# All transposed column pairs of a kernel's second half as seven products of sums, in two passes over token groups

## The chip, the cores and the metric

The kernel runs on one core of one Trainium2 chip. A time is device microseconds from start to end of one execution. The engines are TensorE (PE in the profile; PEld its weight loads), VectorE (DVE), ScalarE (ACT), GpSimd (POOL) and SyncE (SP), whose queue issues nearly all DMA transfers.

## What is computed

One layer of a streaming encoder for 2048 prompt tokens (positions 0 to 2047) and 64 sample tokens of a stream with 4096 past positions, all in float32 with model width 1024:

```
h = rmsnorm(x, norm_g) @ w_in                  # 1024 x 6144 columns: qa ka va za qb kb vb zb (512 each), ga gb (1024 each)
oa = differential attention(rmsnorm(qa), rmsnorm(ka), va)   # 4 heads, two 64-wide halves, chunk mask, linear bias
ob = retention(qb, kb / sqrt(128), vb)         # 4 heads of 128, chunks of 64, a running state
oa = rmsnorm(oa) * (1 - lam_init) * silu(za);  ob = rmsnorm(ob) * silu(zb)
y = x + (sigmoid(ga) * (oa @ w_oa) + sigmoid(gb) * (ob @ w_ob)) @ w_out
```

Keys, values and the retention state are outputs too.

## The kernel before

**Matmuls in parts.** Each float32 operand is kept as a high part in the PE's round float type and a low part, the difference (tiles `xh`, `xl`, `wh`, `wl`); a product is three matmuls, high by high, high by low and low by high. A matmul has 128 x 128 weights and 256, 288 or 512 moving columns. For a weight block, a DMA lands 256 KB in a staging tile `ws` (three of them), ACT casts it to `wh` (L727), and POOL or DVE subtracts to get `wl` (L748). Twelve `w` buffers make six high/low pairs.

**Two halves.** The first half projects 1024 prompt tokens and, for the columns of attention, the sample tokens. The second, which the change touches, has the other 1024 prompt tokens and, for the columns of the pairs, the 64 sample tokens: 1088 columns, taken as two token halves of 544, each in two groups of 256 and 288. The quarters A11, A12, A21, A22 of x are named by token half and by 512-row half of the contraction; S1 to S4 are their sums. x is scaled, transposed and split by the end of the first half and stays in SBUF.

**Columns of the second half.** va, ka, qa and vb are made with tokens on the partitions (`natural`, `mm_group`, L1137). The other 4096 columns make 16 pairs of 128-column blocks, with columns on the partitions, and are stored to DRAM (qbT, kbT, zaT, zbT, gaT, gbT). Eleven of the pairs go through `transposed`, eight block products per pair and group; the last five through `quad` (L1566), phase by phase: for each of seven products, all five pairs, and both token groups with the same weights. A phase's x sum is formed by POOL (`x_again`), stored to DRAM (`xd`), loaded to `xraw` and split by ACT and DVE (`x_pass`, L1527, L1530). Sums of weight blocks were formed in the first half and stored (`wsum`) for these five pairs. The products come out of PSUM as sums: ACT copies (L1593) or DVE adds to an SBUF tile `u` (L1586).

**Beside it.** Attention of both halves (`qk_block` L1880 and L1881; softmax L1889, L1920, L1942; `at_pv` L1970 to L2008) and retention run between the projection's blocks. After the last pair the output follows: gated heads by the two output weights (L2673 to L2679), then the final product (L2801 to L2803). Their weights and inputs are loaded and split during the last pairs.

**What sets the order.** The program is written by a planner of generator tasks with priorities: each keeps clocks of the engines (`self.pe`, `act`, `dve`, `pool`, `dma`) and yields a time or a condition; the planner emits the instruction of the first task that may go. Each engine, and the SP queue, executes in the order of emission. `lighter` gives an operation to DVE or POOL by whose planned clock is behind.

**Small roots.** `rsqrt_small` takes the inverse root of up to 8 values per partition: two ACT operations (L381, L382) and three on DVE (L385 to L387). `rms_t` normalises attention's output; one 1 x 256 cast (L1713) is DVE's.

## Time and profile before

| | |
|---|---|
| times of three runs | 1881.78 to 1882.8 us, median 1882.35 |
| profiled execution, span | 1880.5 us |
| PE busy | 1866.5 us, 99% |
| DVE, ACT, POOL busy | 71%, 52%, 36% |
| DMA | 340.07 MB, mean 181 GB/s |
| granted TensorE clock | 1.000 |

The span runs from the first to the last instruction of the profiled execution. The profile groups instructions by line, engine, operation and tile; a time behind a group is its busy time and the mean of one, or, where three numbers stand with slashes, the least, the median and the largest in ns. A busy PE is not PE at its peak: matmuls overlap, so the spacing of their starts counts, not the duration of one.

### The profile page before, as it was taken

What the parts mean: (1) busy time and instruction counts of PE and PEld (TensorE: products, weight loads), DVE (VectorE), ACT (ScalarE), POOL (GpSimd) and SP (SyncE); (2) the same over time, 40 slices, a digit from 0 to 9 for tenths busy, and PEclk for the clock granted to TensorE, in tenths of its full rate; (3) what the DMA queues carried; (4) which work ended last, traced back from release to release, by engine and by line L of the source; (5) the groups of instructions that cost most, each with busy time, mean ns of one, the idle gap of its engine ahead of it and who ended that gap; (6) DMA issues with size and microseconds to landing.
All of it is one profiled execution on the core that took longest, in us unless ns stands there. A gap on an engine that the chain in (4) does not pass through costs nothing.

```text
span 1880.5 us, 33007 instructions
## 1 busy us (share of the span) xinstructions
PE 1866.5 (99%) x11090; PEld 1645.2 (87%) x11090; DVE 1331.2 (71%) x3112; ACT 975.8 (52%) x2266; POOL 679.2 (36%) x728
## 2 busy tenths in 40 slices
PE   9999999999999999999999999999999999999999
PEld 7788888888888889888988889999999999998887
DVE  6765857558585677787587777677875769887664
ACT  6434545554434566556465655556666446564221
POOL 2420356555552122023210344243224555432442
PEclk9999999999999999999999999999999999999999
DMA  7664555666867967556523659446437988886542
GB/s 257 215 176 125 160 164 171 180 198 196 246 183 192 262 190 191 155 171 173 140 73 96 176 135 244 120 129 155 120 112 234 262 253 249 260 260 216 161 158 77
DMA packets 402555, 340.07 MB, mean 181 GB/s; under 512 B 85329, under 2 KB 348625, under 8 KB 401362
## 3 DMA queue, kind: packets, MB, share of 16 engines
q1 hardware_dynamic: 402386, 337.97, 61.6%
q8 instruction: 87, 1.43, 0.3%
q14 instruction: 82, 0.67, 0.1%
HBM read 218.27 MB, written 118.75 MB: 179 GB/s over the span
## 4 chain that ended last, share of the span: by engine, by line
PE 84%; DMA 6%; DVE 4%; SPq 2%; ACT 1%; issue 1%; POOL 1%; DVEq 0%; ACTq 0%; POOLq 0%
PE mm L1137 30%; PE mm L989 8%; PE tp L989 4%; PE at L1992 3%; PE s L1880 2%; PE s L1881 2%; PE s L989 2%; PE pv L1972 2%; PE pv L1971 2%; PE pv L1970 2%; PE s L2803 1%; PE s L2802 1%; PE s L2801 1%; SPq L280 1%; PE pv L2258 1%
## 5 line engine op out<-in xcount | busy, mean ns | idle before, releaser
L748 POOL TENSOR_TENSOR wl<-ws,wh 128x512 fp32r<-128x512 f32 x107 | 148.1, 1395 | 256.5 <-ACT wh L727 185.2
L1137 PE MATMUL mm<-wh,xh 128*128 128x512 f32 x504 | 203.0, 403 | 0.0
L1137 PE MATMUL mm<-wl,xh 128*128 128x512 f32 x504 | 197.9, 393 | 0.4 <-POOL wl L748 0.4
L1137 PE MATMUL mm<-wh,xl 128*128 128x512 f32 x504 | 198.2, 393 | 0.0
L1137 PE MATMUL mm<-xh,wh 128*128 128x288 f32 (+2 forms) x544 | 179.8, 331 | 0.0
L1137 PE MATMUL mm<-xh,wl 128*128 128x288 f32 (+2 forms) x544 | 175.5, 323 | 0.0
L1137 PE MATMUL mm<-xl,wh 128*128 128x288 f32 (+2 forms) x544 | 175.5, 323 | 0.0
L1920 ACT ACTIVATE row<-row,a_mx 128x1024 f32<-128x1024 f32 (+7 forms) x144 | 149.7, 1042 | 12.0 <-DVE a_mx L1899 12.0
L2008 DVE TENSOR_TENSOR atl<-at,ath 128x512 fp32r<-128x512 f32 (+1 forms) x144 | 92.5, 658 | 77.0 <-ACT ath L2006 76.9
L2006 ACT CAST ath<-at 128x512 fp32r<-128x512 f32 (+1 forms) x144 | 79.2, 565 | 106.5 <-PE at L1992 106.0
L856 POOL TENSOR_TENSOR wl<-ws,wh 128x256 fp32r<-128x256 f32 x64 | 54.9, 858 | 198.0 <-ACT wh L847 197.7
L1747 POOL TENSOR_TENSOR r_y<-r_y,r_sq 128x256 f32<-128x256 f32 x32 | 30.4, 949 | 237.2 <-DVE r_sq L1744 154.1
L1137 PEld LDWEIGHTS mm<-wh,xl 128*128 128x128 f32 x504 | 94.6, 188 | 21.5
L1137 PEld LDWEIGHTS mm<-wl,xh 128*128 128x128 f32 x504 | 95.0, 188 | 18.5 <-POOL wl L748 0.9
L1137 PEld LDWEIGHTS mm<-wh,xh 128*128 128x128 f32 x504 | 94.8, 188 | 17.8 <-DVE raw L1308 0.2
L1137 PEld LDWEIGHTS mm<-xh,wh 128*128 128x128 f32 x544 | 102.4, 188 | 7.2
L1137 PEld LDWEIGHTS mm<-xl,wh 128*128 128x128 f32 x544 | 102.5, 188 | 6.9
L1137 PEld LDWEIGHTS mm<-xh,wl 128*128 128x128 f32 x544 | 102.3, 188 | 6.7
L1889 DVE CUSTOM_DVE_ANT_0 row<-s,dfar 128x512 f32<-128x512 f32 (+2 forms) x141 | 87.0, 628 | 24.0 <-PE s L1881 18.1
L1942 DVE SCALAR_TENSOR_TENSOR row<-row,a_w 128x1024 f32<-128x1024 f32 (+5 forms) x88 | 96.5, 1102 | 0.0
L1880 PE MATMUL s<-K,q 128*128 128x512 f32 (+3 forms) x240 | 90.5, 379 | 1.1 <-DVE a_acc L1889 1.1
L727 ACT CAST wh<-ws 128x512 fp32r<-128x512 f32 x111 | 67.7, 619 | 41.3 <-PE mm L1137 9.8
(543 smaller groups left out, 5959.4 us busy)
## 6 DMA issues: line engine op xcount, KB each, us to landing
ws<-in_w_in_dram SPq DMA_DIRECT2D x155, 256.0 KB, 3.4
q<-qT SPq DMA_DIRECT2D x128, 128.0 KB, 4.0
K<-kT SPq DMA_DIRECT2D x48, 256.0 KB, 4.5
V<-vN SPq DMA_DIRECT2D x24, 512.0 KB, 5.7
...
wz<-in_w_in_dram SPq DMA_DIRECT2D x32, 256.0 KB, 4.1
row<-in_cache_k_T_dram SPq DMA_DIRECT2D x32, 256.0 KB, 3.1
row<-in_cache_v_diff_dram SPq DMA_DIRECT2D x32, 256.0 KB, 3.6
```

Of the source, the lines that this page charges most:

```text
L727: self.nc.scalar.copy(h, st)
L748: eng.tensor_sub(l, st, h.bitcast(F32))
L856: nc.gpsimd.tensor_sub(l[:, cs], src, h[:, cs].bitcast(F32))
L989: nc.tensor.matmul(ps, w[:, c], xs[x][c], start=bool(tag) and c == 0 and i == 0, stop=c == 3 and i == 2, skip_group_check=True)
L1137: nc.tensor.matmul(ps, p, q, start=c == 0 and i == 0, stop=c == KC - 1 and i == 2)
L1880: nc.tensor.matmul(ps, q1s, kk, start=True, stop=False)
L1889: nc.vector.tensor_tensor_reduce(out=row[:, k0:k0 + n], in0=ps, in1=tab, scale=-SLOPES[h], scalar=3.0e38, op0=ALU.add, op1=ALU.min, accum_ ...
L1920: nc.scalar.activation(u, u, AF.Exp, bias=mx, scale=-1.0, accum_out=lp[:, k:k + 1])
L1942: nc.vector.scalar_tensor_tensor(out=u0, in0=u1, scalar=w[:, 0:1], in1=u0, op0=ALU.mult, op1=ALU.add)
L1992: nc.tensor.transpose(at[:, w:w + 128], src, self.ident)
L2006: nc.scalar.copy(ah[:, :w], at[:, :w])
L2008: nc.vector.tensor_sub(al[:, :w], at[:, :w], ah[:, :w].bitcast(F32))
```

## The change

All 16 pairs go through the new `third` (matmuls at L1524 of the changed kernel), in two passes: all pairs for the token group of 256, then all pairs for the group of 288. A pair and group takes seven products of twelve matmuls in the order of the table `THIRD`: the weight block or sum, the x quarter or sum, the accumulator (a to d), and what has to be read out of the accumulator first. Three products are added onto an accumulator that already holds another. Each pass loads, casts and splits all its weight blocks, 224 in all; the sums come from DRAM (`wsum`, now for 16 pairs in eight stores each) straight into the `wl` tile, without a staging tile. Low parts of these blocks are DVE's or POOL's, whichever clock is behind, until the output weights are being prepared (`self.wo` is set), and DVE's from then on.

The four x sums of each group are formed at staging (`x_form`, on DVE or POOL) and stored to `xsum`; x of the second group is stored split to `xg` and its place reused; `x_flow` loads and splits the operands of each pass. va of the second half comes first, as two groups of 256 columns. Retention's second half is started after four pairs of each pass, a part of it each time. `rsqrt_small` becomes one POOL power, and in `rms_t` the L1713 cast goes, with ACT casting the squares in place of squaring twice.

```diff
+THIRD = [("b11", "A11", "a", None, "t_p1"), ("t2", "S2", "b", None, "t_p6"), ("b21", "A12", "a", "p1", "t_p2"),
+         ("t3", "S3", "c", None, "t_p7"), ("t1", "S1", "d", None, "t_p5"), ("t4", "A22", "c", "u3", "t_p4"),
+         ("b22", "S4", "d", "c22", "t_p3")]
+SUMS = ("S1", "S3", "S2", "S4")
 WIDTH = (256, 288)
+HANDOVER = [("S2", 1, 0), ("A12", 0, 0), ("S3", 0, 1), ("S1", 1, 1), ("A22", 0, 2), ("S4", 1, 2)]
...
+        self.wsum = tc.dram_tile([16, 4, 128, 4, 128], F32, name="wsum")
+        self.xsum = tc.dram_tile([2, 4, 128, 4, 288], F32, name="xsum")
+        self.xg = tc.dram_tile([2, 128, 2, KC, 288], F32, name="xg")
...
     def rsqrt_small(self, ms, n, ready):
-        nc = self.nc
-        sp = self.sp
         r = ms.shape[0]
...
-        nc.scalar.activation(y, ms, AF.Ln)
-        nc.scalar.activation(y, y, AF.Exp, scale=-0.5)
-        self.A(n, ready, 40)
-        yield self.A(n, 0.0, 40)
-        nc.vector.scalar_tensor_tensor(out=t, in0=y, scalar=-0.5, in1=y, op0=ALU.mult, op1=ALU.mult)
-        nc.vector.tensor_mul(t, t, ms)
-        nc.vector.scalar_tensor_tensor(out=y, in0=t, scalar=1.5, in1=y, op0=ALU.add, op1=ALU.mult)
-        for _ in range(3):
-            self.tr = self.V(70, self.act)
+        y = self.sp.tile([128, 8], F32, tag="sm_y", name="sm_y")[:r, :n]
+        self.nc.gpsimd.tensor_tensor(y, ms, self.power[:r, :n], op=ALU.pow)
+        self.pool = max(self.pool, ready) + 350 + 165 * n
+        self.tr = self.pool + LAT
+        yield self.tr
...
+    def x_form(self, g, tiles, t):
+        nc = self.nc
+        a11, a12, a21, a22 = tiles
+        yield t
+        for k, (out, one, two, op) in enumerate(((a22, a22, a21, "tensor_add"), (a21, a11, a21, "tensor_sub"),
+                                                 (a11, a22, a11, "tensor_sub"), (a12, a12, a11, "tensor_sub"))):
+            eng, cost = self.lighter()
+            getattr(eng, op)(out, one, two)
+            t = cost(1024, t)
+            self.spawn(self.x_put(g, k, out, t), 1, "w")
+            yield t - LAT - PACE
+
+    def x_put(self, g, k, out, t):
+        yield t + g * k * PARK
+        t = self.st(self.xsum[g, k, :, :, 0:256], out.rearrange("p (c t) -> p c t", c=4), 1 << 19)
...
     def next_load(self, c0, kind):
         for shape, src in self.w_source(c0, kind):
-            yield from self.take("ws")
-            st = self.sb(self.wp, shape, "ws")
-            self.wst.append((st, self.ld(st, src, 1 << 18), shape))
+            st = None
+            if kind != "pair" or src.tensor is self.i["w_in"].tensor:
+                yield from self.take("ws")
+                st = self.sb(self.wp, shape, "ws")
+            wx = kind is True and self.spare
+            tag = yield from self.either(2, "w", *(("wx",) if wx else ()))
+            h, l = (self.sb(self.spare if tag == "wx" else self.wp, shape, tag, n, F32R) for n in ("wh", "wl"))
+            raw = l.bitcast(F32) if st is None else st
+            self.wst.append((raw, st is not None, h, l, self.ld(raw, src, 1 << 18), (tag, tag)))
             yield self.pe
     def next_piece(self, kind):
         self.npiece += 1
         yield lambda: len(self.wst) > 0
...
+        raw, staged, h, l, t, tags = self.wst.pop(0)
         if t > self.pe:
             yield t
-        self.nc.scalar.copy(h, st)
+        self.nc.scalar.copy(h, raw)
         t = self.A(512, max(self.pe, t))
-        if kind is True:
+        if kind is False:
+            new = [[h[:, 0], l[:, 0], None, (), t], [h[:, 1], l[:, 1], None, tags, t]]
+        elif kind is True:
             new = [[h[:, 0], l[:, 0], None, tags, t]]
...
         else:
             new = [[h, l, None, tags, t]]
         self.wq += new
...
+        self.spawn(self.next_low(kind, raw, staged, h, l, t, new), 0, "w")
+        yield self.act - PACE
+    def next_low(self, kind, raw, staged, h, l, t, new):
+        eng, cost = self.nc.gpsimd, self.G
+        if kind == "pair":
+            yield t - LAT
+            eng, cost = self.lighter() if self.wo is None else (self.nc.vector, self.V)
+        eng.tensor_sub(l, raw, h.bitcast(F32))
         t = cost(512, t)
-        self.give("ws", t)
+        if staged:
+            self.give("ws", t)
         for u in new:
             u[2] = t
+        yield self.pe
...
+    def x_flow(self):
+        self.xop, self.xlast = [{}, {}], {}
+        self.passed = False
+        xh, xl = self.xnext[0]
+        yield lambda: len(self.xt_ready) == 8
+        for k, (b, j) in (("A11", (0, 0)), ("A12", (0, 1)), ("A22", (1, 1))):
+            self.xop[0][k] = (*(x[:, b, 4 * j:4 * j + 4] for x in (xh, xl)), 0.0)
+        yield lambda: "kqv11" in self.done
+        for k, x in enumerate(self.xnext[1]):
+            t = self.st(self.xg[k], x.bitcast(F32), 1 << 21)
+        yield lambda: self.seg1_done is not None
+        yield max(self.seg1_done, t + LATE)
+        for k, name in enumerate(("S2", "S1", "S4")):
+            self.spawn(self.x_half(0, name, *(x[:, 1152 * k:1152 * k + 1024] for x in self.xroom[1])), 0, "w")
+        self.x_whole("A11", *(x[:, 3456:4608] for x in self.xroom[1]))
+        yield lambda: "nat1" in self.done
+        yield self.marks["nat1"] + LAT
+        yield from self.x_half(0, "S3", *(x[:, 2048:3072] for x in self.xroom[0]))
+        for name, seg, k in HANDOVER:
+            yield lambda: name in self.xlast
+            yield self.xlast[name]
+            parts = [x[:, 1152 * k:1152 * k + 1152] for x in self.xroom[seg]]
+            if name[0] == "A":
+                self.x_whole(name, *parts)
+            else:
+                self.spawn(self.x_half(1, name, *parts), 0, "w")
+        yield lambda: len(self.xop[1]) == 7
+        self.passed = True
+
+    def x_whole(self, name, h, l):
+        b, j = (int(k) - 1 for k in name[1:])
+        for k, x in enumerate((h, l)):
+            t = self.ld(x.bitcast(F32), self.xg[k, :, b, 4 * j:4 * j + 4].rearrange("p c t -> p (c t)"), 589824)
+        self.xop[1][name] = (*(x.rearrange("p (c t) -> p c t", c=4) for x in (h, l)), t)
+
+    def x_half(self, g, name, h, l):
+        nc = self.nc
+        n = WIDTH[g]
+        raw = l.bitcast(F32)
+        t = self.ld(raw.rearrange("p (c t) -> p c t", c=4), self.xsum[g, SUMS.index(name), :, :, 0:n], 2048 * n)
+        yield t
+        for c in range(2):
+            sl = slice(2 * n * c, 2 * n * c + 2 * n)
+            nc.scalar.copy(h[:, sl], raw[:, sl])
+            t = self.A(2 * n, self.pe)
+            yield t
+            eng, cost = self.lighter()
+            eng.tensor_sub(l[:, sl], raw[:, sl], h[:, sl].bitcast(F32))
+            t = cost(2 * n + 100, t)
+        self.xop[g][name] = (*(x.rearrange("p (c t) -> p c t", c=4) for x in (h, l)), t)
+
+    def third(self, g, dst, d0, scale, grouped, last):
+
+        nc = self.nc
+        n = WIDTH[g]
+        q = {"g": g, "n": n}
+        bank = {}
+        for name, op, b, after, fin in THIRD:
+            yield lambda: len(self.wq) > 0 and self.wq[0][2]
+            wh, wl, t, tags, _ = self.wq.pop(0)
+            yield lambda: op in self.xop[g]
+            xh, xl, tx = self.xop[g][op]
+            if after is None:
+                tag = yield from self.either(1, "mm", *(("tp",) if self.wo is None else ("s", "at")))
+                bank[b] = (self.psum(tag)[:, :n], tag)
+            else:
+                yield lambda: after in q
+                t = max(t, q[after])
+            ps, tag = bank[b]
+            if max(t, tx) > self.pe:
+                yield max(t, tx)
+            for c in range(4):
+                for k, (w, x) in enumerate(((wh, xh), (wh, xl), (wl, xh))):
+                    nc.tensor.matmul(ps, w[:, c], x[:, c], start=after is None and c == 0 and k == 0,
+                                     stop=c == 3 and k == 2, skip_group_check=True)
+                    t = self.P(n)
+                if c == 1:
+                    yield self.pe
+            for tag2 in tags:
+                self.give(tag2, t)
...
+            self.spawn(getattr(self, fin)(q, ps, tag, t, dst, d0, scale, grouped), 0, "w")
             yield self.pe
...
+    def t_p1(self, q, ps, bank, t, dst, d0, scale, grouped):
+        q["a"], tag = q["at"] = yield from self.q_ev(q["n"])
+        yield t
+        q["p1"] = self.q_copy(q["a"], ps, scale, q["n"], t)
+
+    def t_p6(self, q, ps, bank, t, dst, d0, scale, grouped):
+        yield lambda: "p1" in q
+        q["b"], q["bt"] = yield from self.q_ev(q["n"])
+        yield max(t, q["p1"])
+        q["u2"] = t = self.q_scaled(q["b"], ps, q["a"], scale, q["n"], t)
+        self.give(q["at"][1], t)
+        self.give(bank, t)
+
...
+    def t_p7(self, q, ps, bank, t, dst, d0, scale, grouped):
+        yield lambda: "u2" in q
+        q["c"], q["ct"] = yield from self.q_ev(q["n"])
+        yield max(t, q["u2"])
+        q["u3"] = self.q_scaled(q["c"], ps, q["b"], scale, q["n"], t)
+
...
+    def t_p5(self, q, ps, bank, t, dst, d0, scale, grouped):
+        yield lambda: "u3" in q
+        ev, tag, t = yield from self.t_out(q, "c", ps, max(t, q["u3"]), scale)
+        q["c22"] = t
...
-        later = [(vb, lambda half: self.natural(half, self.fin_vb(), False, True), True)]
-        plain = [(c0, lambda half, a=a: self.transposed(*a), False) for c0, a in again[:PLAIN]]
-        c0s, args = zip(*again[PLAIN:])
-        seqs = [first + early + seq, [plain[0], wide[0], plain[1], wide[1], wide[2], m0, m1, plain[2], plain[3],
-                                      *later, (None, "nat"), (None, "ret"), *plain[4:],
-                                      (c0s, lambda half: self.quad(args), "quad")]]
+        later = (vb, lambda half: self.natural(half, self.fin_vb(), False, True, True), True)
+        second = [(va + 256 * g, lambda half, g=g: self.natural(half, self.fin_va(g), True), False) for g in range(2)]
+        second += [*wide[1:], m0, m1, later, (None, "nat")]
+        for g in range(2):
+            for k, (c0, a) in enumerate(again):
+                second.append((c0, lambda half, g=g, a=a, k=k: self.third(g, *a, g == 0 and k == 15), "pair"))
+                if k == 3:
+                    second.append((None, ("ret", "rest")[g]))
+        seqs = [first + early + seq, second]
```

**SP where the second half starts.** Ahead of the first attention loads (K, q and V are attention's operands, ws weights, vN and kT outputs kept in DRAM). Before:

```order
L280 DMA q<-qT_58 64x2x256 x2
L280 DMA ws<-in_w_in_dram 128x2x256
L285 DMA vN_61<-thi 128x512
L285 DMA out_v_prompt_dram<-raw 128x512
L285 DMA vN_62<-tlo 128x512
L285 DMA oaT<-r_o 128x256
```

With the change:

```order
L287 DMA xsum<-row 512x1x256 x2
L287 DMA xsum<-xT 512x1x256 x2
L287 DMA vN_61<-thi 128x2x256
L287 DMA out_v_prompt_dram<-raw 128x2x256
L287 DMA gbT<-ev 128x2x256
L287 DMA vN_62<-tlo 128x2x256
L287 DMA xsum<-row 512x1x256
L282 DMA dnear<-in_c_dnear_dram 128x512
L287 DMA vN_61<-thi 128x2x256
L287 DMA out_v_prompt_dram<-raw 128x2x256
L282 DMA K<-kT_59 64x1024
L282 DMA K<-kT_60 64x1024
```

Stores of the x sums stand between and ahead of these loads.

**SP in the last pairs.** wst are output weights, z and on the output's inputs, gaT and gbT results. Before:

```order
L280 DMA xraw<-xd 128x2176
L280 DMA z<-zaT 128x2x264
L280 DMA on<-oaT 128x2x264
L280 DMA ws<-wsum 128x4x128
L280 DMA z<-zbT 128x2x264
L280 DMA on<-obT 128x2x264
```

With the change:

```order
L282 DMA ws<-in_w_in_dram 128x4x128
L287 DMA gaT<-ev 128x4x8
L287 DMA gaT<-ev 128x256
L282 DMA wst<-in_w_o_ret_dram 128x2x256
L282 DMA ws<-in_w_in_dram 128x4x128
L282 DMA wst<-in_w_o_ret_dram 128x2x256
L282 DMA wl<-wsum 128x512
L287 DMA gbT<-ev 128x4x8
L287 DMA gbT<-ev 128x256
L282 DMA ws<-in_w_in_dram 128x4x128
```

A weight load, of one block, now stands between the stores of every result.

**DVE in the last pairs.** ev and u are evacuations, on the gated heads. Before:

```order
L1586 TENSOR_TENSOR ev<-s,u_16727 128x288
L2479 TENSOR_TENSOR w_o_retl_16953<-wst,w_o_reth_16952 128x2x256
L1586 TENSOR_TENSOR ev<-at,u_16726 128x256
L1586 TENSOR_TENSOR ev<-at,u_16727 128x288
L2479 TENSOR_TENSOR w_o_diffl_16951<-wst,w_o_diffh_16950 128x2x256
L1586 TENSOR_TENSOR ev<-mm,u_16726 128x256
L1586 TENSOR_TENSOR ev<-mm,u_16727 128x288
```

With the change:

```order
L1593 TENSOR_TENSOR ev<-mm,ev 128x288
L770 TENSOR_TENSOR wl<-ws,wh 128x512
L770 TENSOR_TENSOR wl<-wl,wh 128x512
L1593 TENSOR_TENSOR ev<-s,ev 128x288
L770 TENSOR_TENSOR wl<-wl,wh 128x512
L2586 TENSOR_TENSOR on<-on,z 128x528
L1593 TENSOR_TENSOR ev<-at,ev 128x288
L770 TENSOR_TENSOR wl<-wl,wh 128x512
L1593 TENSOR_TENSOR ev<-at,ev 128x288
L2586 TENSOR_TENSOR on<-on,z 128x528
```

Low parts of the weights, before mostly on POOL, now stand between DVE's evacuations.

366 lines of the change are left out of this document (104 added, 262 removed).

## The prediction

> **What bounds the kernel now.** I read the page's busy times and its chain first, then TensorE's waits, then the stretches.
>
> ```profile
> PE 1866.5 (99%) x11090; PEld 1645.2 (87%) x11090; DVE 1331.2 (71%) x3112; ACT 975.8 (52%) x2266; POOL 679.2 (36%) x728
> ...
> PE 84%; DMA 6%; DVE 4%; SPq 2%; ACT 1%; issue 1%; POOL 1%; DVEq 0%; ACTq 0%; POOLq 0%
> ```
> ```profile
> PE at L2679 <- DVE ogl L2630: 1.7, 2, 1.3
> PE tp L1880 <- DMA q<-qT: 1.1, 1, 1.1
> ```
>
> TensorE is busy for 99% of the span, and its longest waits, the two rows above, are 1.7 and 1.1 us. So the time is the number of matmuls times their spacing, and a change gains what it takes from that sum and loses what it adds in waits. Where waits could come is read from the stretches (us; then busy time and instructions of PE, PEld, DVE, ACT, POOL; granted clock, DMA share, GB/s):
>
> ```profile
> 600.00:640.00 40.00, 36.89 (x229) 32.65 (x228) 22.23 (x77) 21.01 (x54) 6.28 (x5) 1.00 1.02 273
> ...
> 1720.00:1760.00 40.00, 40.00 (x175) 32.48 (x174) 33.19 (x41) 13.94 (x24) 19.15 (x12) 1.00 0.69 233
> 900.00:1417.00 517.00, 515.91 (x3397) 471.80 (x3397) 380.64 (x1071) 301.79 (x652) 152.72 (x216) 1.00 0.51 136
> 1417.00:1524.00 107.00, 107.00 (x856) 106.97 (x855) 76.00 (x124) 54.86 (x106) 55.30 (x39) 1.00 0.86 251
> ...
> 1560.00:1600.00 40.00, 40.00 (x330) 40.00 (x330) 36.72 (x64) 24.01 (x62) 22.70 (x20) 1.00 0.75 228
> ...
> 1640.00:1680.00 40.00, 40.00 (x330) 40.00 (x329) 35.99 (x65) 25.93 (x67) 19.16 (x15) 1.00 0.93 285
> ```
>
> Only 600 to 640, where the second half starts, loses PE time (3.1 us), and there the DMA engines are full. DVE at 92% (1560 to 1600) and 285 GB/s (1640 to 1680) cost nothing. The clock is 1.00 throughout.
>
> **TensorE's sum.** The spacing of matmuls comes from the starts in the timeline, for the plain projection and for the seven-product form that five pairs already have:
>
> ```profile
> 684.55 0.39 PE L1137 MATMUL mm<-wh,xl 128*128 128x512 f32 x1
> ...
> 688.03 0.40 PE L1137 MATMUL mm<-wh,xl 128*128 128x512 f32 x1
> ```
> ```profile
> 1433.05 0.28 PE L1566 MATMUL s<-xh,wh 128*128 128x256 f32 x1
> ...
> 1434.46 0.30 PE L1566 MATMUL s<-xh,wh 128*128 128x288 f32 x1
> ...
> 1436.06 0.28 PE L1566 MATMUL at<-xh,wh 128*128 128x256 f32 x1
> ```
>
> Fifteen steps of 512 columns take 3.48 us, 232.0 ns each; in 1720 to 1760, 175 of them give 228.6. I take 230. Twelve steps of 256 columns take 1.41 us, 117.5 ns each; twelve of 288 take 1.60 us, 133.3 each. So a narrow matmul costs a little more per column than a wide one, and the saving is smaller than a count of columns says.
>
> Removed with the eleven plain pairs (24 matmuls to each output block and group): 480 of 512 columns, 1056 of 288, 96 of 256. The first value projection turns 192 of 512 into 384 of 256. The five old product pairs had 420 of 256 and 420 of 288; sixteen now have 1344 of each. Net: 512, minus 672; 256, plus 1212; 288, minus 132. That is -672 x 230 + 1212 x 117.5 - 132 x 133.3 = -154.6 + 142.4 - 17.6 = **-30 us** (-29 at 228.6, -31 at 232.0). The rest of PE's work stays.
>
> **The last stretch.** On PE, attention now ends after 126 of the 224 product blocks, so 98 blocks stand with little beside them, and the last 40 or so with only the output's preparation. The old phases used each weight block for both groups, 24 matmuls or 3.01 us; a block now lasts 12 matmuls, 1.60 us in the second pass, and every weight is loaded, cast and split a second time.
>
> ```profile
> ws<-wsum SPq DMA_DIRECT2D x20, 256.0 KB, 4.9
> ```
> ```profile
> 1462.96 5.85 DMA ws<-wsum
> ```
> ```profile
> L727 ACT CAST wh<-ws x29: 604/620/636, 1420.8 to 1508.7; 128x512 fp32r<-128x512 f32 x29
> ```
> ```profile
> L748 DVE TENSOR_TENSOR wl<-ws,wh x4: 675/687/1453, 1430.8 to 1476.9; 128x512 fp32r<-128x512 f32 x4
> ```
>
> There are six high/low buffer pairs, 6 x 1.60 = 9.6 us round. A trip is landing 4.9, cast 0.62, low part 0.69, use 1.60: 7.8 us, so a landing may be 6.7 us before PE waits. At 261 GB/s one took 5.85, in the chain's row. Between the first output-weight load and the last pair weight, SP's order now has 130 transfers, 23.6 MB, beside 40 x 1.60 = 64 us of PE; before, 89 and 21.8 MB in some 70 us of 1417 to 1524. At the best rate shown, 285 GB/s, 23.6 MB take 83 us. SP says the same:
>
> ```profile
> 1456.16 2.63 SPq L285 DMA_DIRECT2D gbT<-ev  x4
> ...
> 1458.90 0.52 SPq L280 DMA_DIRECT2D ws<-wsum  x1
> ```
>
> At 0.52 to 0.66 us an issue, 130 take 68 to 86 us, and a store that waits for its evacuation holds the weight loads queued behind it. The loads start up to 9.6 us before their block. So the stall is between 0 (loads and stores spread over the earlier blocks) and 83 - 64 = 19 us; I take the middle, **+9**: nothing says that either the spreading or the lateness is complete.
>
> DVE has every low part here: 7 x 0.69 and five evacuations of 0.43 make 7.0 us per pair against 11.2 of PE, for six pairs 42 of 64 us, with ten output-weight low parts (6.9) and some gating 55. It fits, unless POOL runs beside it:
>
> ```profile
> 1455.16 0.71 DVE L1530 TENSOR_TENSOR xl<-xraw,xh 128x544 fp32r<-128x544 f32 x1
> ...
> 1456.16 1.50 DVE L1530 TENSOR_TENSOR xl<-xraw,xh 128x544 fp32r<-128x544 f32 x1
> ...
> 1457.02 1.79 POOL L748 TENSOR_TENSOR wl<-ws,wh 128x512 fp32r<-128x512 f32 x1
> ...
> 1457.58 0.41 DVE L1586 TENSOR_TENSOR ev<-at,u 128x256 f32<-128x256 f32 x1
> ```
>
> A subtraction of two SBUF tiles doubles beside a POOL one, and the evacuation from PSUM doesn't. Sixteen POOL operations of 1.8 us cover 29 of the 64 us, so some 19 of 42 low parts cost 0.8 more: 55 + 15 = 70, 6 us over. That lies within the 0 to 19 and isn't added.
>
> [...]
>
> **Attention with the first pass beside it.** The plain work beside attention was 480 x 230 + 1056 x 133.3 + 96 x 117.5 = 262 us; now it is 112 x 1.41 + 14 x 1.60 = 180, so attention's 517 us become 435. DVE's 380.6 of them gain 18 pair-passes of five evacuations,
>
> ```profile
> L1586 DVE TENSOR_TENSOR ev<-mm,u x14: 406/432/457, 1450.9 to 1525.5; 128x256 f32<-128x256 f32 x7, 128x288 f32<-128x288 f32 x7
> ```
>
> 90 x 0.43 = 38 us, and 25 low parts of 0.7 to 1.5, some 25; they lose about 28 (below, and the old sums' low parts). That is 416 of 435 us, 95%, above the 92% that the trace shows as free. Price: 0 if DVE's lead holds, 22 if the last 5% is never filled; I take **+5**, near the free end, since a stretch at 92% lost nothing.
>
> **The start of the second half.** 4.2 MB of x sums and 4.7 MB of split x are stored between loads that arrive just in time:
>
> ```profile
> 595.53 6.04 DMA q<-qT
> 601.60 4.09 DMA q<-qT
> 605.69 7.50 DMA qbT<-ev
> ```
>
> 8.9 MB at 273 GB/s are 33 us of DMA; about half meets the full 40 us, and the later stretch has room. Price 0 to 16; I take **+4**, because the second group's sums are spread out and stores wait for nobody. The sums' forming replaces 160 small POOL operations of the old re-forming, and POOL is 36% busy: nothing.
>
> **Small roots.** Fifty-one times two ACT and three DVE operations become one POOL power, for which before has no row; the cast goes too.
>
> ```profile
> L382 ACT ACTIVATE sm_y<-sm_y x51: 205/209/212, 78.8 to 1262.6; 128x8 f32<-128x8 f32 x32, 128x4 f32<-128x4 f32 x16, 64x8 f32<-64x8 f32 x2, 64x4 f32<-64x4 f32 x1
> ```
> ```profile
> L386 DVE TENSOR_TENSOR sm_t<-sm_t,ms x51: 154/167/1225, 82.3 to 1263.1; 128x8 f32<-128x8 f32 x32, 128x4 f32<-128x4 f32 x16, 64x8 f32<-64x8 f32 x2, 64x4 f32<-64x4 f32 x1
> ```
> ```profile
> L1713 DVE CAST r_hi<-r_sq x32: 280/282/1107, 621.7 to 1420.7; 1x256 fp32r<-1x256 f32 x32
> ```
> ```profile
> L1747 POOL TENSOR_TENSOR r_y<-r_y,r_sq x32: 725/740/1775, 627.0 to 1429.9; 128x256 f32<-128x256 f32 x32
> ```
>
> 51 x 3 x 0.167 = 26 us leave DVE and 32 x 0.28 = 9 more, about 28 of the 35 beside attention. A power takes between 0.167 (DVE on the same eight values) and, at ten times POOL's 256-value product, 7 us; the shape is small, so I take 1 us. The chain it replaces is 2 x 0.21 + 3 x 0.17 = 0.9 us, and nobody on PE waited for it: **0**. At 7 us, 51 cost POOL 357 us and its low parts would be late (a rival below).
>
> **Sum.** 1880.5 - 30 + 9 + 5 + 4 = 1868.5 us of span. The median, 1882.35, lies 1.85 over the profiled span: **1870 us**.
>
> **Rivals.** (a) All the new waits stay hidden: 1882.35 - 30 = 1852. For it: PE lost nothing at 92% DVE or 285 GB/s. Against it: both limits are now exceeded on the estimates above, for 64 us and longer.
>
> (b) The last stretch is starved: 19 + 5, and the start 8: 1882.35 - 30 + 32 = 1884, no change.
>
> (c) Slower: the accumulators. Three of a pair's seven products go into a bank that ACT or DVE must have read, and between lies one block, 1.41 us. Before, the evacuation came late without harm:
>
> ```profile
> 1455.44 0.27 PE L1566 MATMUL at<-xh,wl 128*128 128x256 f32 x1
> ...
> 1457.58 0.41 DVE L1586 TENSOR_TENSOR ev<-at,u 128x256 f32<-128x256 f32 x1
> ```
>
> From the product's last start to the evacuation's end are 2.55 us, 1.14 more than the cover. There are 32 pair-passes, so 96 such places; some 54 have attention's matmuls between, but the 42 of the last 14 pairs stand alone: at 1.14 each 48 us, 1882.35 - 30 + 48 + 4 = 1904. It decides from 26 / 42 = 0.62 us each. Against it: that row's evacuation stood behind a low part of 1.50 us, which is the exception.
>
> (d) The change doesn't do what it says: the power is near 7 us, or narrow matmuls fed from two passes don't keep 117.5 ns; half the saving gone, 1870 + 15 = 1885.
>
> **How the numbers follow.** Forecast 0.39, (a) 0.21, (b) 0.15, (c) 0.19, (d) 0.06. A difference of 0.2%, 3.8 us, is what a measurement can tell from none: 1878.6 and 1886.1. Faster: the forecast, (a), and a few hundredths of (b), 0.62; same: the rest of (b) and half of (d), 0.16; slower: (c) and the other half, 0.22. The range runs from (a), 1852, to 1894, short of (c). The forecast alone spans 1860 to 1878.
>
> **What would show it.** PE's matmul count up by 408 at unchanged spacing; blocks of 1.41 and 1.60 us. In the last stretch, PE waits named for DVE's low parts, ACT's casts or weight loads, some 9 us in all, with DMA near 285 GB/s; if the waits name evacuations instead, (c) is right. Beside attention, DVE at 90% or more with short waits. The forecast is wrong if PE loses over 28 us, or under 8, in all.

## The result, and the profile after

The changed kernel took 1928.68 us (median of four executions, 1925.45 to 1935.29), the kernel before 1882.41 beside it: 1.0248 times as long, interval 1.0234 to 1.0263. The forecast was 1870, its range 1852 to 1894. It is slower, and the sign was wrong.

The first two rows are the page's busy times and its chain; then come TensorE's longest waits (us in total, times, longest), and four stretches in the columns that the prediction used.

```profile
PE 1869.5 (97%) x11498; PEld 1661.5 (86%) x11498; DVE 1378.1 (71%) x3043; ACT 1016.8 (53%) x2257; POOL 825.8 (43%) x724
...
PE 77%; DVE 10%; DMA 6%; issue 2%; ACT 2%; POOL 2%; SPq 1%; DVEq 0%; ACTq 0%; POOLq 0%
```
```profile
PE s L1844 <- DVE a_acc L1853: 10.7, 10, 5.8
PE mm L1160 <- DVE tlo L1413: 5.2, 1, 5.2
...
PE s L1844 <- DMA q<-qT: 2.6, 1, 2.6
```
```profile
600.00:640.00 40.00, 27.14 (x176) 25.32 (x174) 19.81 (x44) 9.48 (x25) 9.29 (x6) 0.83 0.99 292
640.00:680.00 40.00, 36.19 (x259) 34.09 (x260) 28.02 (x90) 24.98 (x57) 7.04 (x6) 0.96 0.92 242
...
1480.00:1520.00 40.00, 36.11 (x242) 34.97 (x241) 25.68 (x44) 22.91 (x42) 9.61 (x7) 0.91 0.98 286
1520.00:1560.00 40.00, 35.50 (x249) 34.45 (x248) 30.22 (x47) 23.19 (x43) 13.00 (x9) 0.96 1.01 282
```

The number of matmuls rose by 408, as forecast. PE's share fell from 99 to 97%, DVE's share of the chain rose from 4 to 10%, and the granted clock, 1.00 throughout before, is 0.83 in one stretch and 0.91 in another. The spacing that the sum was made with held. In attention, beside the first pass, and in the last pairs:

```profile
1137.94 0.28 PE L1524 MATMUL mm<-xh,wh 128*128 128x256 f32 x1
...
1139.36 0.28 PE L1524 MATMUL tp<-xh,wh 128*128 128x256 f32 x1
...
1435.78 0.29 PE L1524 MATMUL mm<-xh,wl 128*128 128x288 f32 x1
...
1437.38 0.29 PE L1524 MATMUL mm<-xh,wl 128*128 128x288 f32 x1
```

Twelve steps take 1.42 and 1.60 us, against 1.41 and 1.60 before. So TensorE's own work did get shorter by about 30 us, and what is slower is what it loses between.

**Where it loses.** I put all matmuls of the program in their order, each at the undisturbed spacing of its form, and compared that with the starts in the trace. What the difference grows by in a stage is what TensorE lost there, by waiting or by a low clock. *Start* is the stage in which the second half begins (trace time about 590 to 760 of the changed kernel), *attention* the stage in which attention runs beside the pairs (about 900 to 1440), *last pairs* the pairs behind it (to about 1570). In us:

| | start | attention | last pairs | elsewhere | all |
|---|---|---|---|---|---|
| before | 4.4 | 2.7 | -0.3 | 16 | 23 |
| after | 28.6 | 31.9 | 15.4 | 22 | 98 |

75 us more are lost: 24 at the start, 29 beside attention, 16 in the last pairs, 6 elsewhere, of which some 5 fall in the first 100 us. 75 - 30 = 45, and 46.3 were measured.

### The profile page after: what moved, and what is told of

Read it like the earlier page. It is cut to its first block, busy times and chain, and to the rows that moved or that the text cites. A ratio compares the mean times of both kernels' runs of the same rounds, so it can differ in the third digit from the quotient of the medians.

```text
span 1927.7 us, 34579 instructions
## 1 busy us (share of the span) xinstructions
PE 1869.5 (97%) x11498; PEld 1661.5 (86%) x11498; DVE 1378.1 (71%) x3043; ACT 1016.8 (53%) x2257; POOL 825.8 (43%) x724
## 4 chain that ended last, share of the span: by engine, by line
PE 77%; DVE 10%; DMA 6%; issue 2%; ACT 2%; POOL 2%; SPq 1%; DVEq 0%; ACTq 0%; POOLq 0%
PE mm L1160 13%; PE mm L1012 9%; PE mm L1524 8%; PE tp L1012 4%; PE at L1956 2%; PE s L1012 2%; DVE row L1853 2%; PE tp L1524 2%; PE s L1844 2%; DMA ws<-in_w_in_dram 2%; PE s L1845 2%; DVE row L1906 2%; PE pv L1936 1%; DMA wl<-wsum 1%; PE pv L1935 1%
## 5 line engine op out<-in xcount | busy, mean ns | idle before, releaser
L1160 PE MATMUL mm<-wh,xh 128*128 128x512 f32 (+1 forms) x568 | 217.8, 384 | 7.4 <-DVE tlo L1413 5.2
L1160 PE MATMUL mm<-wl,xh 128*128 128x512 f32 (+1 forms) x568 | 211.6, 373 | 2.3 <-POOL wl L770 2.3
L1160 PE MATMUL mm<-wh,xl 128*128 128x512 f32 (+1 forms) x568 | 211.5, 372 | 0.0
L1524 PE MATMUL mm<-xh,wh 128*128 128x256 f32 (+1 forms) x660 | 195.2, 296 | 7.8 <-DVE ev L1593 3.2
L1524 PE MATMUL mm<-xh,wl 128*128 128x256 f32 (+1 forms) x660 | 191.1, 290 | 1.2 <-DVE wl L770 0.7
L1524 PE MATMUL mm<-xl,wh 128*128 128x256 f32 (+1 forms) x660 | 190.9, 289 | 0.0
L770 POOL TENSOR_TENSOR wl<-wl,wh 128x512 fp32r<-128x512 f32 x86 | 122.7, 1431 | 128.9 <-ACT wh L753 107.3
L381 POOL TENSOR_TENSOR sm_y<-ms,power 128x8 f32<-128x8 f32 (+3 forms) x51 | 76.3, 1496 | 172.3 <-DVE ms L1346 55.0
L1524 PEld LDWEIGHTS mm<-xh,wh 128*128 128x128 f32 x660 | 125.9, 191 | 14.5 <-ACT wh L753 3.8
L1524 PEld LDWEIGHTS mm<-xl,wh 128*128 128x128 f32 x660 | 126.0, 191 | 3.0
L1524 PEld LDWEIGHTS mm<-xh,wl 128*128 128x128 f32 x660 | 126.2, 191 | 1.7 <-DVE wl L770 0.9
L753 ACT CAST wh<-wl 128x512 fp32r<-128x512 f32 x128 | 78.4, 621 | 55.4 <-DMA wl<-wsum 50.2
```

Source lines behind the costliest of these rows:

```text
L381: self.nc.gpsimd.tensor_tensor(y, ms, self.power[:r, :n], op=ALU.pow)
L753: self.nc.scalar.copy(h, raw)
L770: eng.tensor_sub(l, raw, h.bitcast(F32))
L1160: nc.tensor.matmul(ps, p, q, start=c == 0 and i == 0, stop=c == KC - 1 and i == 2)
L1524: nc.tensor.matmul(ps, w[:, c], x[:, c], start=after is None and c == 0 and k == 0, stop=c == 3 and k == 2, skip_group_check=True)
```

## The experiments

Every run has one profiled execution, and unless a ratio is given one time. Four executions of the changed kernel lie 10 us apart, so I read a single run by its stages more than by its time. These are the losses of all runs, worked out as above:

| run | start | attention | last pairs | time, us |
|---|---|---|---|---|
| start_neither | 9.2 | 36.9 | 16.2 | 1916.4 |
| start_noform | 10.2 | 35.2 | 14.4 | 1911.0 |
| stores_of_x | 26.0 | 32.9 | 16.8 | 1927.0 |
| form_on_dve | 29.6 | 21.3 | 15.9 | 1927.9 |
| no_acc_wait | 28.0 | 33.4 | 13.4 | 1926.9 |
| evac_on_act | 27.0 | 29.0 | 14.9 | 1923.3 |
| no_sum_lows | 26.7 | 16.5 | 17.4 | 1914.1 |
| lows_on_dve | 26.7 | 25.6 | 18.6 | 1922.0 |
| lows_on_dve_no_sums | 28.2 | 19.4 | 18.7 | 1917.4 |
| evac_on_act_no_sum_lows | 27.5 | 20.8 | 16.9 | 1918.9 |
| both_causes | 10.8 | 20.7 | 14.9 | 1902.5 |
| no_sum_loads_2 | 28.1 | 35.5 | 8.4 | 1922.4 |
| no_sum_no_wo_loads | 29.7 | 35.6 | 15.1 | 1934.0 |
| prep_on_pool | 26.6 | 36.8 | 14.2 | 1964.6 |
| last_lows_shared | 26.2 | 38.2 | 20.6 | 1941.6 |
| old_roots | 33.0 | 34.8 | 20.3 | 1946.2 |
| three_undone | 29.7 | 38.1 | 5.9 | 1930.2 |
| before_pow | 5.7 | 4.3 | 1.7 | 1884.7 |

Two things have to be known to read this table. First, TensorE's order of matmuls is the changed kernel's own in all runs but form_on_dve, the two lows_on_dve, old_roots and three_undone; in these five attention stands elsewhere among the pairs, so their columns compare less well. Second, a single execution scatters. Up to 1488 us prep_on_pool and last_lows_shared give TensorE, DVE, ACT and POOL the same work in the same order as the changed kernel, and beside attention they lose 36.8 and 38.2 against its 31.9. Runs whose edit leaves the start alone lose 26.2 to 29.7 there, and the changed kernel and those whose edit leaves the last pairs alone 14.4 to 16.8.

### The start of the second half

**No sums formed, none stored.** The operands of the passes are loaded from x itself.

```diff
-            getattr(eng, op)(out, one, two)
...
-        t = self.st(self.xsum[g, k, :, :, 0:256], out.rearrange("p (c t) -> p c t", c=4), 1 << 19)
+        t = self.pe + (1 << 19) / 150.0 + DMA_LAT
...
```


> The changed kernel without forming the x sums at staging and without storing them (their later loads read other data of the same size, so the sums are left out of the computation). Theory A (the sums' forming and storing cost the start): the 28 us that TensorE loses between 580 and 760 us fall below 8, the time from 1929 to about 1905 to 1910. Rival (the start is slow for its other new transfers: split x stored, value projection in two groups, K and q loads): the loss stays above 20 and the time above 1920.

**Not formed, but stored** (what is stored is not summed): the first of the two edits alone.

> The changed kernel with the stores of the x sums kept, but the eight additions and subtractions ahead of them left out (unformed tiles are stored). If DVE and POOL in each other's way are what delays the start (DVE's last x splits took 1.7 us each beside POOL's sums, and SP waited 9.6 us for POOL's results), the loss between 580 and 760 falls by 10 us or more, to under 18, and the time to about 1915. If the 4.2 MB of stores on a full DMA are, it falls by less than 5 and the time stays above 1922.

The loss at the start falls from 28.6 to 9.2 without both (below 8 was forecast) and to 10.2 without the forming alone. Eight operations cost about 18 us, and 4 MB of stores about one, which is within the scatter. First a stretch of the run without the forming; then the timeline (start, us, operation) of DVE before, of DVE and of POOL after, and of DVE without the forming:

```profile
600.00:640.00 40.00, 36.60 (x283) 34.08 (x282) 21.83 (x72) 20.03 (x49) 9.15 (x7) 1.00 0.93 261
```
```profile
587.75 4.89 DVE L563 TENSOR_TENSOR xl<-row,xh 128x512 fp32r<-128x512 f32 x8
```
```profile
591.55 13.80 DVE L558 TENSOR_TENSOR xl<-row,xh 128x512 fp32r<-128x512 f32 x8
...
605.88 0.68 DVE L1413 TENSOR_TENSOR tlo<-mm,thi 128x512 fp32r<-128x512 f32 x1
```
```profile
593.00 2.73 POOL L572 TENSOR_TENSOR row<-xT,row 128x1024 f32<-128x1024 f32 x1
595.81 2.73 POOL L572 TENSOR_TENSOR xT<-row,xT 128x1024 f32<-128x1024 f32 x1
```
```profile
589.02 5.60 DVE L558 TENSOR_TENSOR xl<-row,xh 128x512 fp32r<-128x512 f32 x8
...
595.14 0.67 DVE L1412 TENSOR_TENSOR tlo<-mm,thi 128x512 fp32r<-128x512 f32 x1
```

The eight subtractions that split x take 13.80 us, 1.72 each, where they take 0.70 without the forming and 0.61 before: POOL forms sums at that moment. The low part `tlo` behind them starts at 605.88 instead of 595.14, 8.2 us of it by the splits, and TensorE's 5.2 us of waiting are for it.

The longest wait of the stage is another one: 5.8 us until 628.75, for `a_acc` (the first row of the waits above). DVE's first operation on attention's scores (L1853) stands in its queue behind a `tlo`, and DVE is idle for 10.81 us ahead of that one (the brackets say for what):

```profile
627.80 0.69 DVE L1413 TENSOR_TENSOR tlo<-mm,thi 128x512 fp32r<-128x512 f32 x1 [10.81 <-ACT raw L1411]
628.41 0.28 DVE L1853 CUSTOM_DVE_ANT_0 row<-s,dnear 128x128 f32<-128x128 f32 x1
```

ACT in turn was idle for 10.43 us until a store from an older `thi` tile had landed, at 626.6; SP had issued that store at 621.76, behind the q loads. So TensorE waits here for a DVE that has nothing to do, through three queues. Without the forming this wait is 0.3 us.

**Is it SP's queue?** A sum's store waits for its forming, up to 3.9 us in the changed kernel's trace, and holds what is behind it. Here the sums are formed, but the stores take a tile of x that is ready.

```diff
-        t = self.st(self.xsum[g, k, :, :, 0:256], out.rearrange("p (c t) -> p c t", c=4), 1 << 19)
+        t = self.st(self.xsum[g, k, :, :, 0:256], self.xnext[g][0][:, 0, 0:4, 0:256].bitcast(F32), 1 << 19)
```


> The changed kernel in which the stores of the x sums take tiles that are ready early (the split x) in place of the sums; the sums are formed as before, on DVE and POOL, and not used. SP's queue is no longer held by a store that waits for a sum. The loss between 580 and 760 us was 28 in the changed kernel, 10 without the forming, 29 with the forming on DVE. Theory I (the store that waits holds SP, and with it the outputs' stores and attention's loads): the loss falls to under 15. Rival J (the engines' work itself: DVE's x splits and what waits for them come late): it stays above 22.

26.0 are still lost, hardly less than the 26.2 to 29.7 of runs that leave this stage alone: no. Only the wait for `a_acc` gets shorter, 3.4 us instead of 5.8.

**Is it POOL beside DVE alone?** All eight sums on DVE.

```diff
-            eng, cost = self.lighter()
+            eng, cost = self.nc.vector, self.V
```


> The changed kernel with the eight operations that form the x sums all on DVE instead of half on POOL. The loss between 580 and 760 us was 28 with them and 10 without them. Theory G (the loss comes from POOL's long operations beside DVE's x splits, each of which took 1.7 us instead of 0.7): it falls to under 18, though DVE gets some 5 us more. Rival H (the forming is simply too much work at that place): it stays at 25 or more.

The splits are quick again, 0.73 us each, and nothing is gained (29.6). DVE's timeline of this run:

```profile
590.45 4.38 DVE L558 TENSOR_TENSOR xl<-row,xh 128x512 fp32r<-128x512 f32 x6
594.75 1.21 DVE L572 TENSOR_TENSOR row<-row 128x1024 f32<-128x1024 f32 x1
...
597.70 0.68 DVE L1413 TENSOR_TENSOR tlo<-mm,thi 128x512 fp32r<-128x512 f32 x1
598.29 1.21 DVE L572 TENSOR_TENSOR row<-xT,row 128x1024 f32<-128x1024 f32 x1
```

```profile
PE s L1844 <- DMA q<-qT: 6.9, 1, 6.9
```

Eight times 1.21 us, the last at 608.57, now stand among the `tlo`, whose results become v, k and q, and in TensorE's waits (the last row) the first q comes late in place of the `tlo`. So the work itself has no room at this place, on either engine. The table bears it out: three runs without the forming lose 9.2 to 10.8 at the start, all others of the changed kernel 26.0 to 33.0.

### Beside attention

**The accumulators**, the prediction's case for slower. The three readings that a block waits for take other data, so on the chip no matmul waits for an accumulator to be read, while the planner's order stays (`q_one` is one DVE operation of the same size that does not read PSUM).

```diff
-        q["p1"] = self.q_copy(q["a"], ps, scale, q["n"], t)
+        q["p1"] = self.q_copy(q["a"], self.ident[:, 0:1].to_broadcast([128, q["n"]]), scale, q["n"], t)
...
-        q["u3"] = self.q_scaled(q["c"], ps, q["b"], scale, q["n"], t)
+        q["u3"] = self.q_one(q["c"], q["b"], q["n"], t)
...
```


> The changed kernel in which the three evacuations that an accumulator's next product waits for don't read the accumulator (a constant or an SBUF tile is read in its place, on the same engines; the sums lose these terms). Rival E (accumulators): the loss between 900 and 1440 falls from 30 to under 14 and in the last stretch too. Theory D (POOL against DVE): it stays above 22, less only what the waits on evacuations by name show (about 6 us).

33.4 against 31.9 to 38.2 beside attention, 13.4 against 14.4 to 16.8 in the last pairs: it is not the accumulators.

**DVE's evacuations** go to ACT as copies without the addition.

```diff
-            self.nc.vector.tensor_add(out, ps, add)
+            self.nc.scalar.copy(out, ps)
...
```


> The changed kernel with the 160 evacuations that DVE adds done as plain copies by ACT at the same place in the order (the additions are left out). DVE loses 69 us of work, ACT gains some 55. Theory B (DVE's load beside attention makes the waits): TensorE's loss between 900 and 1440 us falls from 30 to under 12, the time to about 1905. Rival (one block of cover is too short for an accumulator that has to be read, whoever reads it): the loss stays above 22 and the time above 1920.

29.0 against 31.9 to 38.2: DVE is relieved by 27 us (rows below), and little comes of it.

**The low parts of the weight sums are left out** (`wl` keeps the whole sum): four of a pair's seven weight blocks are sums.

```diff
-        eng.tensor_sub(l, raw, h.bitcast(F32))
+        if staged:
+            eng.tensor_sub(l, raw, h.bitcast(F32))
```


> The changed kernel without the low parts of the 128 weight sums (their subtraction is left out; the tile keeps what was loaded). This takes 86 of POOL's 1.4 us operations and 42 of DVE's away, and with them the two engines' collisions; accumulators, loads and casts stay. So far the 30 us that TensorE loses between 900 and 1440 us did not go with 160 of DVE's operations (they went to 26). Theory D (POOL's low parts hold up DVE's operations on SBUF tiles, and these hold up what TensorE waits for): the loss falls to under 15. Rival E (one block of cover is too short for an accumulator that has to be read): it stays above 22. In the last stretch (1440 to 1570, 16 us lost) the loss stays if late loads make it, and falls under 8 if DVE's low parts do.

16.5, half of the loss. Of 125 low parts of the pairs between 900 and 1360 us the changed kernel's POOL makes 120 and DVE 5; here POOL makes 55 and DVE 1. So it is mostly POOL that has less to do, and DVE's operations get shorter by it: the same 1084 of them in this stage, low parts aside, take 493.5 us (the sum of their durations) in the changed kernel, 492.3 to 496.6 in stores_of_x, prep_on_pool and last_lows_shared, and 465.8 here.

**All low parts on DVE**, so POOL does not run beside it; and the same with the sums' low parts left out.

```diff
-            eng, cost = self.lighter() if self.wo is None else (self.nc.vector, self.V)
+            eng, cost = self.nc.vector, self.V
```


> The changed kernel with all low parts of the pairs on DVE, also beside attention. DVE gets about 120 more operations; POOL loses them. Theory D: DVE's own work grows by 60 us or so, but its operations on SBUF tiles don't double any more; the loss between 900 and 1440 stays about the same or falls by some us (20 to 32). If DVE's sheer load sets it (380 + 60 and more of 460 us), it grows to over 45, and the time to over 1940.

> The changed kernel without the low parts of the weight sums (left out) and with the other pairs' low parts all on DVE, so that POOL has none beside attention. No low parts of the sums took the loss between 900 and 1440 us from 30 to 13; POOL still had 55 low parts there. Theory D (POOL's low parts against DVE's operations): the loss falls to under 9, although DVE gets some 55 operations more. Rival F (what is left comes from the DVE work of attention and evacuations itself): it stays at 12 or rises.

25.6 and 19.4: DVE's mere load, which was to bring over 45, is not the bound. DVE's longest softmax operation shows what POOL's company costs (ns, least, median, largest; after, and all on DVE):

```profile
L1906 DVE SCALAR_TENSOR_TENSOR row<-row,a_w x57: 605/1359/2309, 906.4 to 1356.1; 128x1024 f32<-128x1024 f32 x29, 128x1152 f32<-128x1152 f32 x4, 128x1280 f32<-128x1280 f32 x4, 128x384 f32<-128x384 f32 x4
```
```profile
L1906 DVE SCALAR_TENSOR_TENSOR row<-row,a_w x49: 599/1270/1754, 903.5 to 1349.3; 128x1024 f32<-128x1024 f32 x24, 128x1152 f32<-128x1152 f32 x4, 128x1280 f32<-128x1280 f32 x4, 128x384 f32<-128x384 f32 x4
```

The largest falls from 2309 to 1754 ns. The medians mix widths; among the 1024-wide ones the median stays at 1.28 us, and the mean falls from 1.48 to 1.30. POOL's company is not new, for before the largest was 2292 ns; there is more of it: 212.4 us of POOL's work in the stretch shown below instead of 139.1. 25.6 is 6 us below the changed kernel, as much as the scatter, and TensorE's order is another one here. With 19.4 where under 9 was forecast, POOL's low parts are not all that is left.

**Evacuations on ACT and no low parts of sums**, the two edits above together.

> The changed kernel without the low parts of the weight sums and with the 160 adding evacuations as plain copies on ACT (both left out of the computation). Alone the first took the loss between 900 and 1440 us from 30 to 13, the second from 30 to 26. Theory K (every operation that the change adds to the queues beside attention has its share, whatever its engine): the loss falls to under 11. Rival L (what is left of 13 us comes from how the blocks stand between attention's matmuls, not from the added work): it stays at 12 to 14.

20.8, no better than the second edit alone. Here is one stretch of 460 us in before, after, evac_on_act, no_sum_lows and lows_on_dve, in this order (busy PE, PEld, DVE, ACT, POOL):

```profile
900.00:1360.00 460.00, 458.91 (x3001) 418.20 (x3001) 341.31 (x977) 267.06 (x584) 139.12 (x206) 1.00 0.52 139
```
```profile
900.00:1360.00 460.00, 442.22 (x3268) 413.82 (x3267) 405.59 (x1036) 315.30 (x648) 212.38 (x160) 1.00 0.61 175
```
```profile
900.00:1360.00 460.00, 444.29 (x3312) 418.88 (x3311) 378.16 (x956) 341.11 (x741) 220.28 (x164) 1.00 0.62 177
```
```profile
900.00:1360.00 460.00, 451.96 (x3395) 428.27 (x3394) 384.97 (x1045) 320.59 (x660) 119.72 (x96) 1.00 0.63 181
```
```profile
900.00:1360.00 460.00, 444.22 (x3315) 420.27 (x3314) 422.83 (x1106) 303.46 (x625) 44.28 (x37) 1.00 0.63 184
```

Neither DVE's busy time nor POOL's goes with the loss. With DVE at 422.8 us (92%) TensorE is idle for 15.8 us, with 405.6 (88%) for 17.8, with 378.2 and with 385.0 for 15.7 and 8.0. What lowers the loss each time is having fewer low parts to make, whoever makes them: the four runs without the sums' low parts (both_causes, below, among them) lose 16.5 to 20.8, all others of the changed kernel 21.3 to 38.2. Each against the same run with them, 6 to 15 us are gained, a fourth to a half. The width of the other span is not explained: runs with the changed kernel's order of matmuls reach from 29.0 to 38.2, and only form_on_dve (21.3) and lows_on_dve (25.6), with another order, lie below. What is left without those low parts, 14 to 18 us over before, I could not settle.

**Both causes at once:** no forming, no low parts of sums.

> Leaves out the four sums of x at staging (what is stored as a sum is the unsummed x) and the low parts of the weight sums. Each alone brought the time to 1911.0 us and 1914.1 us, from 1928.7: TensorE lost 10.2 instead of 28.6 us at the start, and 16.5 instead of 31.9 us beside attention. Theory P (two separate causes, each with its own stage): start 10, attention 16, last pairs 15, time about 1896 us. Theory Q (work that is late in one stage only comes later: what one edit gives, the other has given too): attention stays over 28 us with the start at 10, time 1908 us or more. In both the kernel stays over the 1882 us of the kernel before, by the last pairs and by what is left beside attention.

10.8 and 20.7, 1902.5 us. The gains stand beside each other, though 6 us short of the sum; the account in which one lateness only shows in two places falls. Even so it is 20 us slower than before.

### The last pairs

**Fewer transfers.** In the second pass no weight sum is loaded (a constant tile is split in its place, so casts and low parts stay); then the output weights are not loaded either.

```diff
+            if st is None and self.nth > 16:
+                raw = self.ident.unsqueeze(1).to_broadcast([128, 4, 128])
+                self.dma = max(self.dma, self.pe) + (1 << 18) / 300.0
...
```


> The changed kernel in which the second pass doesn't load its 64 weight sums (16.8 MB; a constant tile is cast and subtracted in their place). If the last stretch is starved by loads, its 16 us fall to under 5, and the time to about 1917; if by DVE's or ACT's order, it stays above 12. Before 1300 us nothing changes.

> The changed kernel in which neither the second pass's 64 weight sums nor the 16 output-weight tiles are loaded (a constant is split in their place, so both are left out of the computation). Of 16 us lost between 1440 and 1570, 8 went with the sums' loads alone. Theory M (transfers and SP's issues in the last stretch): under 4 are left. Rival N (ACT's and DVE's order in that stretch): 7 or more are left.

8.4, and then 15.1 again with still less to transfer. The rows are the second run's stretches and TensorE's waits in them:

```profile
1480.00:1520.00 40.00, 34.06 (x229) 32.92 (x228) 26.71 (x40) 21.40 (x41) 12.51 (x9) 0.91 0.61 162
1520.00:1560.00 40.00, 36.03 (x266) 35.18 (x265) 35.10 (x50) 22.71 (x45) 13.25 (x9) 1.00 0.65 168
```
```profile
PE at L1530 <- DVE wl L776: 3.0, 2, 2.3
PE mm L1530 <- ACT wh L759: 2.3, 2, 1.4
PE mm L1530 <- DVE ev L1599: 1.6, 1, 1.6
```

With the DMA engines at 0.61 instead of 0.98, TensorE loses as much in this run, waiting for casts, low parts and evacuations. So full transfers are not needed for the loss. But in the changed kernel itself the loads of the sums do come late: ACT's casts of them stand idle for 16.8 us between 1440 and 1580 until they land, and in the chain from 1490 to 1560 they have the largest share:

```profile
by line: DMA wl<-wsum 28.2%; PE at L1524 19.9%; PE s L1524 18.1%; PE mm L1524 12.9%; DMA on<-obT 7.1%; DVE wl L770 3.9%; issue 3.1%; DMA gaT<-ev 3.1%; ACT wh L753 1.9%; ACT L2583 1.6%; ACT z L2583 0.9%; DVE ev L1593 0.6%; ACT ev L1600 0.6%;
```

The first run, which leaves out just these loads, is 6 us below the scatter of this stage, and the second, which leaves out more, is within it. TensorE's order is the same in both. Late loads are thus a part of what is seen in the changed kernel, and how much of the 16 us they carry stays open.

**The output's preparation off DVE.** In these stretches the output weights' low parts and the gated heads stand in DVE's queue ahead of the pairs' work. Here POOL has them.

```diff
-        if on_pool:
+        if on_pool or tag == "oz":
...
-        nc.vector.tensor_mul(on, on, z)
-        t = self.V(n + 100, t)
+        nc.gpsimd.tensor_mul(on, on, z)
+        t = self.G(n, t)
...
-        nc.vector.tensor_sub(l, on, h.bitcast(F32))
-        t = self.V(n + 100, t)
+        nc.gpsimd.tensor_sub(l, on, h.bitcast(F32))
+        t = self.G(n, t)
```


> Computes the reference. The output's preparation (the low parts of the output weights, the gating of the heads and its low parts) is given to POOL, so that in the last pairs DVE's queue holds the pairs' own low parts, splits and evacuations alone. Theory R (TensorE's 15 us there are lost because these operations stand in DVE's queue ahead of the pairs' work): 5 us or less lost in the last pairs, time about 1918 us. Theory S (ACT's casts, or the collision of POOL with DVE, are what ends last): the loss stays between 12 and 20 us, time 1924 to 1933 us.

**The pairs' low parts shared to the end.**

```diff
-            eng, cost = self.lighter() if self.wo is None else (self.nc.vector, self.V)
+            eng, cost = self.lighter()
```


> Computes the reference. The pairs' low parts stay shared between DVE and POOL to the end, instead of being DVE's alone once the output weights are prepared. If DVE is simply too full in the last pairs (some 70 of 64 us by the forecast's upper count), POOL takes a part and the loss falls from 15 to 8 us or less; if POOL's operations slow DVE's as much as they relieve it, it stays between 12 and 20 us. Time 1921 us against 1924 to 1933 us.

14.2 and 20.6: nothing is gained by either. These runs don't separate a relief of DVE from a collision with POOL: between 1440 and 1580 DVE's low parts of the pairs take 1.07 and 1.06 us on the mean instead of 0.76, so DVE's busy time falls only from 88.5 to 84.5 and 85.8 us. The first run loses 36 us more behind the pairs, where the output now waits for POOL, as its waits show:

```profile
PE s L2645 <- POOL ogl L2596: 15.6, 10, 3.7
```

In the changed kernel the waits of this stage have no one owner (trace time 1440 to 1580):

```profile
PE mm L1524 <- ACT ev L1600: 2.2, 1, 2.2
PE mm L1524 <- DVE ev L1593: 1.9, 1, 1.9
PE at L1524 <- ACT wh L753: 1.5, 1, 1.5
```

So the cause of the 16 us stays open here. The lowest loss of the table, 5.9 in three_undone, comes with another order: there attention's last score matmul is at 1499 us instead of 1341, so attention's matmuls still stand between the late pairs.

### The small roots

**The power alone, in the kernel before:**

```diff
-        nc.scalar.activation(y, ms, AF.Ln)
...
+        self.nc.gpsimd.tensor_tensor(y, ms, self.power[:r, :n], op=ALU.pow)
```


> The kernel before with one part of the change alone: the small roots as one POOL power. The power took 1.5 us in the changed kernel, against some 0.9 for the chain before, so each of 51 roots comes 0.6 us later, and TensorE's gap of 2.1 us at 84 us, with the low clock behind it, stands behind a root. Theory C: 3 to 6 us slower than before (1885 to 1889). Rival: the roots are covered and DVE is relieved of 26 us: within 2 us of before.

1884.68 against 1882.36 us, ratio 1.0012 (1.0002 to 1.0021): two us, if anything. One power takes 1.50 us on the mean, in the changed kernel's groups:

```profile
L381 POOL TENSOR_TENSOR sm_y<-ms,power 128x8 f32<-128x8 f32 (+3 forms) x51 | 76.3, 1496 | 172.3 <-DVE ms L1346 55.0
```

**The old roots in the changed kernel:**

> The changed kernel with the small roots as before (two ACT and three DVE operations). Alone on the kernel before, the power cost 2.3 us. Theory C: the gap at 84 us with the low clock behind it goes (60 to 100 us: from 4 us lost to about 1), and 2 to 5 us in all: 1923 to 1927. Rival: DVE's 26 us more beside attention cost as much as the power did: 1927 to 1932.

1946.2 us, slower than with the power, by a few us in each of several stages, and above both forecasts. The gap at 84 us, which was put down to the power, doesn't go either: TensorE waits 2.3 us there with the old roots, and the clock is 0.80 and 0.78 behind it, while the kernel before with the power has 0.3. So the roots don't carry the 46 us. Whether the old ones are dearer here, or the order that follows is only worse, one run can't tell.

**Three parts undone:** all sums and all low parts on DVE, old roots.

> The changed kernel with the x sums formed on DVE, all pairs' low parts on DVE, and the old small roots. If the parts add up: low parts on DVE gave 7 us, the forming 8 to 14, the roots 3: 1904 to 1911, still slower than before, because the last stretch (15 to 18 us lost) and what is left beside attention (some 20) stay. If the DVE becomes the bound with all three: 1915 or more.

1930.18 us, ratio 1.0265 (1.0239 to 1.0292), the changed kernel's own time again: 9 us less in the last pairs, and 38.1 beside attention, the upper end of the scatter. Moving the added work between engines didn't pay here. None of the complete versions beats the kernel before.

## Why the prediction was wrong

**TensorE's sum** was right: 408 more matmuls at the spacing forecast, -30 us.

**The start**, +4 with bounds 0 to 16, measured 24. The step that failed is "the sums' forming replaces 160 small POOL operations of the old re-forming, and POOL is 36% busy: nothing". It priced the forming by a share of the whole span. The old operations were spread over the phases; the new ones stand within some 20 us, directly ahead of the `tlo` that make v, k and q, in the one stretch of the second half that already lost PE time. Forming cost 18 of the 24, the transfers that I did price about 1, and 5 are open. "Stores wait for nobody" was wrong too: SP waited 3.9 us for one of POOL's sums, which cost little by itself.

**Attention**, +5 with bounds 0 to 22, measured 29. The step that failed is "near the free end, since a stretch at 92% lost nothing", and with it the upper bound, which held only what DVE would have over its capacity. DVE came to 88%, less than the 95% forecast, and the loss came all the same. The sum had 25 low parts as DVE's and nothing for what POOL's company does to DVE's other operations; it was priced for the last pairs alone. POOL made 120 of 125, and those of the sums alone lengthened DVE's other operations by 28 us. The waits are short and spread over several tiles (after, 900 to 1440):

```profile
PE s L1844 <- DVE a_acc L1853: 4.9, 9, 1.2
PE pv L2374 <- DVE row L2368: 3.0, 2, 2.1
PE pv L1936 <- DVE atl L1972: 2.5, 4, 0.9
```

I read them so (argued, not shown): a result on which TensorE depends comes late from DVE, because what stands ahead of it in DVE's queue has become longer, and a busy share doesn't show this. What the runs do show is that splitting the weight sums makes a fourth to a half of the loss, and that DVE's operations are longer with it.

**The last stretch**, +9 with bounds 0 to 19, measured 16. The size is within its bounds, and the step, transfers beside too little PE time, is neither borne out nor refuted: weight sums land late in the changed kernel, and without their loads 8.4 is lost, but with 162 to 168 GB/s instead of 282 to 286 another run loses as much as the changed kernel. The prediction had counted DVE at 55 to 70 of 64 us and left that inside the term; the waits are for DVE and ACT. DVE's shares in the two stretches, 64 and 76%, show that DVE is late and not full. The pair of rows by which it priced POOL's company, 0.71 against 1.50 us, is not one alone and one beside POOL: a POOL operation of 1.90 us started 0.01 us after the first of the two subtractions, which kept its 0.71 us. The one that started while POOL was at work took 1.50.

**The roots** were priced at 0 by 1 us an operation. It is 1.50, and 2 us in all on the kernel before, so this term was small, as priced.

**The rivals.** The only one that forecast slower, the accumulators, gave 1904 by a mechanism that the run without these waits refutes. The prediction said it would be wrong if PE lost over 28 us in all; PE lost 75 more than before. Each stage was judged alone, at a middle or near its free end. Two of the three came out over their upper ends, and even these ends together, 16 + 22 + 19 = 57, would have given 1882 - 30 + 57 = 1909, outside the range. And a part of the price of several waits was missing: the clock, 0.83, 0.91 and 0.96 in the stretches of 40 us shown.
